# HGRN2 scores: four small levels joined in two groups of four blocks, single-key terms multiplied on GpSimd, four raw weight buffers in place of five

## The chip, the cores and the metric

One core of one Trainium2 chip runs the whole program. The metric is device time in microseconds of one launch. A core has five engines that run on their own and meet by semaphores: PE (TensorE, matmul), DVE (VectorE), ACT (ScalarE), POOL (GpSimd) and SP (SyncE, which here only issues DMAs). Each engine takes its instructions strictly in the order in which they stand in its own stream, and so does the queue of DMAs that SP issues.

## The reference, cut to what matters

A decoder layer: one combined input projection, two token mixers (mLSTM and HGRN2), a gated merge, an output projection with layer norm, and a SwiGLU feed-forward with layer norm. 512 tokens, width 1024, float32. The change is in the HGRN2 mixer: eight heads, a state of 128 keys by 128 values each.

```
def step(state, xs):                      # chunks of 16 tokens
    qc, kc, vc, lfc = xs
    a = jnp.cumsum(lfc, axis=2)
    rel = jnp.where(causal, a[:, :, :, None, :] - a[:, :, None, :, :], -jnp.inf)
    scores = jnp.einsum('bhtk,bhtsk,bhsk->bhts', qc, jnp.exp(rel), kc)
    o = (jnp.einsum('bhts,bhsv->bhtv', scores, vc)
         + jnp.einsum('bhtk,bhkv->bhtv', qc * jnp.exp(a), state))
    ...
```

Written without chunks: the score of query token t on key token s is the sum over the 128 keys of q[t] k[s] times the product of the forget gates f between s and t. The output of a head is scores times values.

## The kernel before, in words

**Weights.** Every projection takes its weight in blocks of 512 KB. `load_w` (L92) has SP issue a DMA into a raw buffer, tag `wraw`, of which there are five. `split` (L88) turns a raw block into a rounded high part `whi` (ACT) and a low remainder `wlo` (DVE), three buffers of each, and `mm3` (L83) makes three matmuls of every product: high by high, low by high, high by low. These are lines L84 to L86. A projection of 128 outputs (`proj_sub`) is 24 matmuls of 512 columns, and `natural_half` is 48 of 256 columns. The raw buffer comes free when its split is done, the split can be made when a `whi` and `wlo` pair is free, so the weight of a projection is split three projections ahead of its use.

**HGRN2 by pairs of heads.** `h_units` computes for a pair of heads (a unit, four in all) the gates f, keys K = 1 - f, queries Q, values v and output gates. K and Q are kept with the 128 keys on the partitions. `h_chain` then computes the scores of that pair while PE runs the projections of the next pair: its steps wait in a list (`defer`, `tick`), and every projection of about 5.5 us counts one tick. Eight ticks make a unit. After the last unit the gate projections of the merge take the place of the next unit.

The scores come by levels that double. Level hs joins two neighbouring blocks of hs tokens: the queries of the second block meet the keys of the first. Ahead of a level all K are multiplied by the gates up to the end of their block, and all Q by those from the start of theirs, so a level is one plain product of K and Q. After a level `h_advance` (L588) multiplies the second half of Q and the first half of K on by the block totals `tot` (L592, L593) and forms the totals of the doubled blocks (L596). The chain is:

- `h_direct_0`, `_1`, `_2`, `_3`: the diagonal and the levels of 1 and 2 tokens. There a product per key and token is formed on DVE (`h_terms`, L571, tile `e`), split into `eh` (ACT) and `el` (DVE), and summed over the 128 partitions by a matmul with ones (`h_sum`, L579).
- `h_level` for 4, 8, 16 and 32 tokens: eight matmuls of 64 columns each (L646; every float32 matmul runs as two instructions in the trace), placed into the score tile `ad` by a predicated copy on DVE (`h_place`, L604, levels 4 and 8) or by copies on ACT (L673, levels 16 and 32).
- `h_level` for 64 (L651), 128 (L657) and 256 tokens (L663).
- `h_out`: the scores times v (L692), the sum of squares of each row on ACT (tile `junk`, whose tag `sg` it shares with other small tiles), a power on POOL (L698), a scaling on DVE (L700), and one tick later the transposes (L705).

**What sets the order.** The steps are written into the program at their ticks; a scheduler then fixes the stream of each engine at build time. On the chip a late operand holds its engine and all that stands behind it there.

**After HGRN2.** `w_proj_b`, then `natural_pass` over `w_out` in two passes of eight blocks (two token tiles each, 12 matmuls of 512 columns for one block), then the feed-forward. Pool `lp` is opened after the HGRN2 pool is closed, on memory that the HGRN2 tiles held. It takes the layer norm's rows (`lng`, `lnb`) and the residual `z`, which SP loads (L756, L757, L827).

Of the kernel before, what the change touches and what calls it, by code (L numbers as in the profile page):

```python
# [29 lines left out]
O_HQ, O_HF, O_HI, O_HG, O_GA, O_GB = 8200, 9224, 10248, 11272, 12296, 13320  # L30
SOFF = [0, 512, 896, 1152]
SCOLS = 1280
WRAW = 5


@with_exitstack
def tile_hybrid_trunk(
# [40 lines left out]
    rp = pool(ctx, "rp", side="right")  # L78
# [9 lines left out]
    def split(src, hi, lo):  # L88
        return nc.scalar.copy(hi, src), nc.vector.tensor_sub(lo, src, hi.bitcast(F32))  # L89

    def load_w(src, kk, nn):
        raw = rp.tile([P, kk, nn], F32, tag="wraw", name="wraw", bufs=WRAW)  # L92
        nc.sync.dma_start(raw, src.rearrange("(k p) n -> p k n", p=P))
        return raw

# [76 lines left out]
    px = pool(st_m, "px", bufs=2, space=PSUM)  # L172
# [7 lines left out]
    for i in range(2):  # L180
        raw = mp.tile([P, 4, 264], F32, tag="dt", name="rawv", bufs=MH)
# [273 lines left out]
    for h in range(MH):  # L455
# [4 lines left out]
        for c in range(4):  # L460
            kk, qq = [feature_chunk(h, c, w) for w in range(2)]
# [16 lines left out]
        vh, vl, _ = vt_  # L478
# [34 lines left out]
    for key, gs_, w in (((1, 0), 2, 1), ((2, 0), 4, 2), ((2, 1), 4, 2), (4, 8, 4), (8, 16, 8)):
        a, n = (key[1], 1) if isinstance(key, tuple) else (0, w)
        m = hp_.tile([P, P // gs_, w], F32, name=f"mask{gs_}{a}")
        nc.gpsimd.memset(m, 1.0)
# [10 lines left out]
    def h_units(pr):  # L527

        st = dict(pr=pr, ad=ads[pr % 2])
        for name in ("f", "K", "Q", "og"):  # L530
            st[name] = hp_.tile([P, 2, T], F32, tag=name, name=name, bufs=2)
        st["v"] = hp_.tile([P, NT, 256], F32, tag="v", name="v", bufs=2)
        st["tot"] = hp_.tile([P, 1024], F32, tag="tot", name="tot", bufs=1)
        f, K, Q, og, v = (st[k] for k in ("f", "K", "Q", "og", "v"))
        for c in range(2):
            n = 2 * pr + c
            wh, wl = fetch(in_cols(O_HF + n * P), KD, P)
            ps = proj_sub(wh, wl, 0, xh, xl)
            nc.scalar.activation(f[:, c], ps, AF.Sigmoid, bias=bcol(O_HF + n * P))
            nc.scalar.activation(K[:, c], ps, AF.Sigmoid, bias=nfcol(n), scale=-1.0)  # L540
            nc.vector.tensor_scalar(f[:, c], f[:, c], omcol(n), lbcol(n), op0=OP.mult, op1=OP.add)
            nc.vector.tensor_scalar_mul(K[:, c], K[:, c], omcol(n))
# [12 lines left out]
        for g in range(2):
            nc.vector.tensor_add(v[:, 2 * g:2 * g + 2], vps[g], vb[:, None, :].to_broadcast([P, 2, 256]))
        tick()
        for c in range(2):
            n = 2 * pr + c
            wh, wl = fetch(in_cols(O_HG + n * P), KD, P)  # L560
            ps = proj_sub(wh, wl, 0, xh, xl)
            nc.scalar.activation(og[:, c], ps, AF.Sigmoid, bias=bcol(O_HG + n * P))
            tick()
        return st

    def h_terms(in0, in1, shape):
# [33 lines left out]
    def h_place(st, ps, gs_, w, key):  # L600

        dst = st["ad"].rearrange("p j (g k) -> p j g k", k=gs_)[:, :, :, gs_ - w:]
        msk = masks[key].bitcast(U32)[:, None].to_broadcast([P, 8, P // gs_, w])
        nc.vector.copy_predicated(dst, msk, ps.rearrange("p j (g k) -> p j g k", k=w))  # L604
# [27 lines left out]
    def h_direct_3(st):  # L632
        pss = [h_sum(parts, 64) for parts in st["e"]]
        for a in range(2):
            h_place(st, pss[a], 4, 2, (2, a))

    def h_level(st, hs):

        K, Q, ad = st["K"], st["Q"], st["ad"]
        if hs < 64:  # L640
            lps = psum(px, "px", (P, 8, 64))
            for c in range(2):
                for j in range(NT):
                    js = slice(j * P, (j + 1) * P)
                    mov = Q[:, c, js].rearrange("p (g two h) -> p g two h", two=2, h=hs)[:, :, 1]
                    nc.tensor.matmul(lps[:, 4 * c + j], K[:, c, js], mov, start=True, stop=True)  # L646
        elif hs == 64:
            lps = psum(px, "px", (P, 8, 64))
            for c in range(2):
                for j in range(NT):  # L650
                    nc.tensor.matmul(lps[0:64, 4 * c + j], K[:, c, j * P:j * P + 64], Q[:, c, j * P + 64:(j + 1) * P],  # L651
                                     start=True, stop=True)
        elif hs == 128:
            lps = psum(px, "px", (P, 2, 2, P))
            for c in range(2):
                for b in range(2):
                    nc.tensor.matmul(lps[:, c, b], K[:, c, 2 * b * P:(2 * b + 1) * P],  # L657
                                     Q[:, c, (2 * b + 1) * P:(2 * b + 2) * P], start=True, stop=True)
        else:
            for c in range(2):  # L660
                lps = psum(px, "px", (P, 2, 256))
                for b in range(2):
                    nc.tensor.matmul(lps[:, b], K[:, c, b * P:(b + 1) * P], Q[:, c, 256:512],  # L663
                                     start=True, stop=True)
# [3 lines left out]
        if hs < 16:
            h_place(st, lps, 2 * hs, hs, hs)
        elif hs < 64:  # L670
            for g in range(64 // hs):
                rows_ = slice(2 * hs * g, 2 * hs * g + hs)
                nc.scalar.copy(ad[rows_, :, 2 * hs * g + hs:2 * hs * (g + 1)], lps[rows_, :, hs * g:hs * (g + 1)])  # L673
        elif hs == 64:
# [52 lines left out]
    for n in range(2, KD):  # L727
        sg = hp_.tile([P, T], F32, tag="sg", name="sga", bufs=2)
# [187 lines left out]
```

## Time and profile before

| | |
|---|---|
| time, median of 3 runs | 1333.22 us (1332.94 to 1334.21) |
| the profiled execution | 1334.2 us, span 1332.5 us |
| granted TensorE clock, mean | 0.997 |
| busy: PE / DVE / ACT / POOL | 1315.9 / 753.9 / 537.0 / 41.2 us |
| HBM read, written | 138.09 MB, 2.10 MB |

The span is what the profile records from the first to the last instruction; 1.7 us lie around it. Busy time of PE counts from the start to the modelled end of a matmul, and neighbouring matmuls overlap, so the pitch from start to start is what a matmul costs in a row of them.

### The profile page before, as it was taken

What the parts mean: (1) busy time and instruction counts of PE and PEld (TensorE: products, weight loads), DVE (VectorE), ACT (ScalarE), POOL (GpSimd) and SP (SyncE); (2) the same over time, 40 slices, a digit from 0 to 9 for tenths busy, and PEclk for the clock granted to TensorE, in tenths of its full rate; (3) what the DMA queues carried; (4) which work ended last, traced back from release to release, by engine and by line L of the source; (5) the groups of instructions that cost most, each with busy time, mean ns of one, the idle gap of its engine ahead of it and who ended that gap; (6) DMA issues with size and microseconds to landing.
All of it is one profiled execution on the core that took longest, in us unless ns stands there. A gap on an engine that the chain in (4) does not pass through costs nothing.

```text
span 1332.5 us, 17405 instructions
## 1 busy us (share of the span) xinstructions
PE 1315.9 (99%) x7023; PEld 1136.1 (85%) x7023; DVE 753.9 (57%) x1140; ACT 537.0 (40%) x811; POOL 41.2 (3%) x78
## 2 busy tenths in 40 slices
PE   8999999999999999999999999999999999999997
PEld 7788889888988998889898988887898888888885
DVE  5764656566555755557586754345765433334575
ACT  4773553444342533332424333323773222233332
POOL 0000000000000002000000000000000000000001
PEclk9999999999999999999999999999999999999999
DMA  8222333233323323332232222235664343335672
GB/s 235 80 72 79 88 88 92 75 81 94 88 79 89 86 79 84 98 96 70 63 83 64 71 72 64 79 95 201 197 186 128 95 129 101 102 95 162 192 229 81
DMA packets 189424, 141.31 MB, mean 106 GB/s; under 512 B 5728, under 2 KB 178592, under 8 KB 189344
## 3 DMA queue, kind: packets, MB, share of 16 engines
q1 hardware_dynamic: 188288, 140.17, 37.0%
q8 instruction: 55, 0.90, 0.3%
q14 instruction: 25, 0.20, 0.0%
q10 hardware_dynamic: 1056, 0.03, 0.0%
HBM read 138.09 MB, written 2.10 MB: 105 GB/s over the span
## 4 chain that ended last, share of the span: by engine, by line
PE 97%; DVE 1%; ACT 1%; DMA 1%; issue 0%; POOL 0%; SPq 0%; DVEq 0%; POOLq 0%
PE pp L84 19%; PE pp L85 19%; PE pp L86 19%; PE pf L84 10%; PE pf L85 10%; PE pf L86 10%; PE px L646 2%; PE px L692 1%; PE s L85 1%; PE s L86 1%; PE s L84 1%; PE px L579 1%; DMA xn<-in_x_dram 1%; PE px L424 1%; PE px L663 1%; PE px L84 0%
## 5 line engine op out<-in xcount | busy, mean ns | idle before, releaser
L89 ACT CAST whi<-wraw 128x1024 fp32r<-128x1024 f32 x246 | 258.1, 1050 | 592.3 <-PE pp L85 253.8
L89 DVE TENSOR_TENSOR wlo<-wraw,whi 128x1024 fp32r<-128x1024 f32 x246 | 300.6, 1223 | 272.4 <-ACT whi L89 270.0
L84 PE MATMUL pp<-xh,whi 128*128 128x512 f32 x704 | 278.1, 395 | 0.0
L86 PE MATMUL pp<-xh,wlo 128*128 128x512 f32 x704 | 275.5, 391 | 0.0
L85 PE MATMUL pp<-xl,whi 128*128 128x512 f32 x704 | 275.4, 391 | 0.0
L86 PEld LDWEIGHTS pp<-xh,wlo 128*128 128x128 f32 x704 | 132.6, 188 | 28.3 <-issue 0.4
L84 PEld LDWEIGHTS pp<-xh,whi 128*128 128x128 f32 x704 | 132.7, 188 | 27.6 <-issue 1.0
L85 PEld LDWEIGHTS pp<-xl,whi 128*128 128x128 f32 x704 | 132.6, 188 | 26.2
L86 PE MATMUL pf<-x1h,wlo 128*128 128x512 f32 (+1 forms) x416 | 148.4, 357 | 0.8 <-DVE wlo L89 0.8
L84 PE MATMUL pf<-x1h,whi 128*128 128x512 f32 (+1 forms) x416 | 148.4, 357 | 0.0
L85 PE MATMUL pf<-x1l,whi 128*128 128x512 f32 (+1 forms) x416 | 148.3, 356 | 0.0
L84 PE MATMUL pp<-whi,xh 128*128 128x256 f32 x352 | 100.6, 286 | 0.0
L85 PE MATMUL pp<-wlo,xh 128*128 128x256 f32 x352 | 99.8, 284 | 0.0
L86 PE MATMUL pp<-whi,xl 128*128 128x256 f32 x352 | 99.5, 283 | 0.0
L86 PEld LDWEIGHTS pf<-x1h,wlo 128*128 128x128 f32 x416 | 78.6, 189 | 12.1 <-DVE wlo L89 1.0
L84 PEld LDWEIGHTS pf<-x1h,whi 128*128 128x128 f32 x416 | 78.6, 189 | 11.3
L85 PEld LDWEIGHTS pf<-x1l,whi 128*128 128x128 f32 x416 | 78.6, 189 | 11.3
L357 DVE SCALAR_TENSOR_TENSOR y<-u,cols,y 128x512 f32<-128x512 f32 x96 | 71.9, 750 | 6.1 <-ACT y L355 2.6
L85 PE MATMUL pf<-wlo,g 128*128 128x512 f32 x176 | 68.6, 390 | 0.0
L86 PE MATMUL pf<-whi,g 128*128 128x512 f32 x176 | 68.5, 389 | 0.0
L84 PE MATMUL pf<-whi,g 128*128 128x512 f32 x176 | 68.4, 389 | 0.0
L85 PEld LDWEIGHTS pp<-wlo,xh 128*128 128x128 f32 x352 | 67.5, 192 | 0.1
(251 smaller groups left out, 1940.3 us busy)
## 6 DMA issues: line engine op xcount, KB each, us to landing
wraw<-in_w_in_dram SPq DMA_DIRECT2D x110, 512.0 KB, 3.9
wraw<-in_w_ffn_down_dram SPq DMA_DIRECT2D x44, 512.0 KB, 3.6
wraw<-in_w_ffn_gate_dram SPq DMA_DIRECT2D x26, 512.0 KB, 3.9
wraw<-in_w_ffn_up_dram SPq DMA_DIRECT2D x26, 512.0 KB, 3.9
wraw<-in_w_proj_a_dram SPq DMA_DIRECT2D x16, 512.0 KB, 3.5
wraw<-in_w_out_dram SPq DMA_DIRECT2D x16, 512.0 KB, 3.8
wraw<-in_w_proj_b_dram SPq DMA_DIRECT2D x8, 512.0 KB, 4.3
xn<-in_x_dram SPq DMA_DIRECT2D x4, 512.0 KB, 5.0
```

Source lines behind the costliest of these rows:

```text
L84: nc.tensor.matmul(ps, lh, rh, start=start, stop=False, **kw)
L85: nc.tensor.matmul(ps, lh, rl, start=False, stop=False, **kw)
L86: nc.tensor.matmul(ps, ll, rh, start=False, stop=stop, **kw)
L89: return nc.scalar.copy(hi, src), nc.vector.tensor_sub(lo, src, hi.bitcast(F32))
L357: nc.vector.scalar_tensor_tensor(y, u[:, tap:tap + T], cwcol(tap, ch), y, op0=OP.mult, op1=OP.add)
L424: nc.tensor.transpose(tps[:, i * P:(i + 1) * P], hn[:, i, c * P:(c + 1) * P], ident)
L579: nc.tensor.matmul(ps.rearrange("p j n -> p (j n)"), ones_r, part.rearrange("p a b -> p (a b)"), start=(i == 0), stop=(i == 1))
L646: nc.tensor.matmul(lps[:, 4 * c + j], K[:, c, js], mov, start=True, stop=True)
L663: nc.tensor.matmul(lps[:, b], K[:, c, b * P:(b + 1) * P], Q[:, c, 256:512], start=True, stop=True)
L692: nc.tensor.matmul(ops[:, i], at, vc(j), start=(e == 0), stop=(e == len(terms) - 1))
```

## The change

1. **Groups.** The levels 4 and 8 become one step `h_group(4)`, the levels 16 and 32 become `h_group(16)`. A group takes four neighbouring blocks of hs tokens. K and Q stand at the state of level hs. The six pairs of blocks (target, source) need Q with the totals of none, one or two blocks between them: `h_group_targets` writes these six variants of Q into a tile `mv` (one copy on ACT, two multiplies on DVE), and the group is eight matmuls of 6 x 32 = 192 columns over four PSUM tiles. Twelve predicated copies on DVE place the result, with masks made once on POOL. Q, K and the totals are then carried over two levels at once. The copies of levels 16 and 32 on ACT are gone.
2. **Times of the steps.** Targets at ticks 3.5 and 5, groups at 4.5 and 6, the levels 64, 128 and 256 at 7, 7.5 and 8 (before 5.5, 6, 6.5), `h_out` at 8.5 and 9 (before 7 and 7.5). So `h_out` of a unit now falls on the ninth tick, where the chain of the next unit has its first: its scores times v stand on PE right ahead of the first sums of `h_direct_1` of the next unit.
3. **Terms on GpSimd.** The multiply of `h_terms` moves from DVE to POOL: five multiplies of 128 x 512 in a unit, two in `h_direct_0`, one in `h_direct_1`, two in `h_direct_2`. Its product takes the tag `sg`; `eh`, `el` share a new tag `w3` (two buffers) with `mv`.
4. **Raw buffers.** Four raw weight buffers. Once pool `lp` exists, every fifth load goes to a buffer in that pool.

```diff
-WRAW = 5
+WRAW = 4
...
+    more, loads = [], [0]
+
     def load_w(src, kk, nn):
-        raw = rp.tile([P, kk, nn], F32, tag="wraw", name="wraw", bufs=WRAW)
+        loads[0] += 1
+        if more and loads[0] % (WRAW + 1) == 0:
+            raw = more[0].tile([P, kk, nn], F32, tag="wmore", name="wraw", bufs=1)
+        else:
+            raw = rp.tile([P, kk, nn], F32, tag="wraw", name="wraw", bufs=WRAW)
...
     def h_terms(in0, in1, shape):
 
-        e = hp_.tile(shape, F32, tag="e", name="e", bufs=2)
-        eh = hp_.tile(shape, FR, tag="eh", name="eh", bufs=2)
-        el = hp_.tile(shape, FR, tag="el", name="el", bufs=2)
-        nc.vector.tensor_mul(e, in0, in1)
+        e = hp_.tile(shape, F32, tag="sg", name="e", bufs=2)
+        w3 = hp_.tile([P, 3] + shape[1:], FR, tag="w3", name="w3", bufs=2)
+        eh, el = w3[:, 0], w3[:, 1]
+        nc.gpsimd.tensor_mul(e, in0, in1)
         split(e, eh, el)
         return eh, el
...
+    def h_group_targets(st, hs):
+
+        qv = st["Q"].rearrange("p c (g b h) -> p b (c g) h", b=4, h=hs)
+        tv = st["cur"].rearrange("p (g b) -> p b g", b=4)
+        ng = 2 * T // (4 * hs)
+        tb = lambda b, n=1: tv[:, b:b + n, :, None].to_broadcast([P, n, ng, hs])
+        mv = hp_.tile([P, 6, 2 * P], F32, tag="w3", name="mv", bufs=2)
+        mvv = mv.rearrange("p b (g h) -> p b g h", h=hs)
+        nc.scalar.copy(mvv[:, 0:3], qv[:, 1:4])
+        nc.vector.tensor_mul(mvv[:, 3:5], qv[:, 2:4], tb(1, 2))
+        nc.vector.tensor_mul(mvv[:, 5:6], mvv[:, 4:5], tb(1))
+        st["mv"] = mv
+
+    def h_group(st, hs):
+
+        K, Q, ad, mv = st["K"], st["Q"], st["ad"], st["mv"]
...
+        for j2 in range(4):
+            lps = psum(px, "px", (P, 6, 2, 32))
+            lpss.append(lps)
+            for j in range(2):
+                t = 2 * j2 + j
+                nc.tensor.matmul(lps[:, :, j], K[:, t // 4, t % 4 * P:(t % 4 + 1) * P], mv[:, :, t * 32:(t + 1) * 32],
+                                 start=True, stop=True)
+        nc.vector.tensor_mul(qv[:, 1:2], qv[:, 1:2], tb(0))
+        nc.vector.tensor_mul(qv[:, 2:3], mvv[:, 3:4], tb(0))
+        nc.vector.tensor_mul(qv[:, 3:4], mvv[:, 5:6], tb(0))
+        nc.vector.tensor_mul(tv[:, 2], tv[:, 2], tv[:, 3])
+        nc.vector.tensor_mul(tv[:, 1], tv[:, 1], tv[:, 2])
+        nt_ = st["tot"][:, st["toff"]:st["toff"] + ng]
+        nc.vector.tensor_mul(nt_, tv[:, 0], tv[:, 1])
...
+        nc.vector.tensor_mul(kv[:, 0:3], kv[:, 0:3], tb(1, 3))
+        for j2 in range(4):
...
+            for b0, b1, d0 in ((0, 3, 1), (3, 5, 2), (5, 6, 3)):
+                nc.vector.copy_predicated(dst[:, d0:4], msk[:, b0:b1], src[:, b0:b1])
...
-        steps += [(t, lambda st, hs=hs: h_level(st, hs)) for t, hs in
-                  ((3.5, 4), (4, 8), (4.5, 16), (5, 32), (5.5, 64), (6, 128), (6.5, 256))]
-        steps += [(7 + 0.5 * c, lambda st, c=c: h_out(st, c)) for c in range(2)]
+        steps += [(t, lambda st, hs=hs: h_group_targets(st, hs)) for t, hs in ((3.5, 4), (5, 16))]
+        steps += [(t, lambda st, hs=hs: h_group(st, hs)) for t, hs in ((4.5, 4), (6, 16))]
+        steps += [(t, lambda st, hs=hs: h_level(st, hs)) for t, hs in ((7, 64), (7.5, 128), (8, 256))]
+        steps += [(8.5 + 0.5 * c, lambda st, c=c: h_out(st, c)) for c in range(2)]
+        steps.sort(key=lambda s_: s_[0])
...
     lp = pool(ctx, "lp", side="right")
+    more.append(lp)
```

**Three places in the streams.** First DVE in `h_direct_1` and `h_direct_2` of a middle unit, before the change. L571 is the multiply of the terms, `el` the low part of their split, L592 and L593 the advance of Q and K, L604 a placement.

```order
L89 TENSOR_TENSOR el<-e,eh 128x512 [waits Activation_49]
L622 COPY_PREDICATED ad_4702<-ident,px 128x512 [waits PE_49]
L89 TENSOR_TENSOR el<-e,eh 128x512 [waits Activation_49]
L571 TENSOR_TENSOR e<-K,Q 128x512 [waits DVE_49]
L89 TENSOR_TENSOR wlo<-wraw,whi 128x1024 [waits DMAHW3_49]
L592 TENSOR_TENSOR Q<-Q,tot 128x256x2 [waits DVE_49]
L593 TENSOR_TENSOR K<-K,tot 128x256x2
L604 COPY_PREDICATED ad_4702<-mask_4680,px 128x512 [waits PE_49]
```

The same place after the change, from the scaling of `h_out` (L749) to the second `el` of `h_direct_2`; `w_...` are tiles of tag `w3`, L607, L608 and L619 are the old L592, L593 and L604, L755 is the old L706.

```order
L749 TENSOR_TENSOR on<-px,sm 128x512 [waits Pool_49]
L89 TENSOR_TENSOR w_6169<-e,w_6169 128x512 [waits Activation_49]
L607 TENSOR_TENSOR Q<-Q,f 128x512
L608 TENSOR_TENSOR K<-K,f 128x512
L607 TENSOR_TENSOR Q<-Q,tot 128x256x2 [waits DVE_49,Pool_49]
L89 TENSOR_TENSOR w_6217<-e,w_6217 128x512 [waits Activation_49]
L608 TENSOR_TENSOR K<-K,tot 128x256x2 [waits DVE_49]
L619 COPY_PREDICATED ad_4720<-mask_4680,px 128x512 [waits PE_49]
L556 TENSOR_SCALAR f<-f,lbw 128x512 [waits Activation_49]
L755 SCALAR_TENSOR_TENSOR og<-px,cols,og 128x512 [waits PE_49]
L557 TENSOR_SCALAR K<-K,lbw 128x512 [waits Activation_49]
L89 TENSOR_TENSOR w_6222<-e,w_6222 128x512 [waits Activation_49]
```

The advance of Q now waits for POOL, since POOL reads the old Q, and the two low parts of `h_direct_2` stand behind it. What POOL does there (L586 the multiplies, L747 the power of `h_out`):

```order
L747 TENSOR_TENSOR sm<-sm,nhalf 128x4 [waits DVE_49]
L586 TENSOR_TENSOR e<-K,Q 128x512 [waits Activation_49,Pool_49]
L747 TENSOR_TENSOR sm<-sm,nhalf 128x4 [waits DVE_49]
L586 TENSOR_TENSOR e<-K,Q 128x512 [waits DVE_49,Activation_49,Pool_49]
L586 TENSOR_TENSOR e<-K,Q 128x512 [waits Activation_49]
```

The second power, for which DVE's L749 waits, now stands behind the multiply of `h_direct_1`. Before, POOL held nothing but the powers here.

The second place is SP's queue at the passage from `w_proj_b` to `w_out`, before and after:

```order
L93 DMA wraw<-in_w_proj_b_dram 128x8x128 x8
L93 DMA wraw<-in_w_out_dram 128x1024 x8
L756 DMA lng<-in_ln_g_dram 128x1024
L757 DMA lnb<-in_ln_b_dram 128x1024
L827 DMA z<-in_x_dram 128x1024 x2
L93 DMA wraw<-in_w_out_dram 128x1024 x8
```

Now the same stretch of the changed kernel's queue:

```order
L99 DMA wraw<-in_w_proj_b_dram 128x8x128 x8
L99 DMA wraw<-in_w_out_dram 128x1024 x4
L808 DMA lng<-in_ln_g_dram 128x1024
L809 DMA lnb<-in_ln_b_dram 128x1024
L879 DMA z<-in_x_dram 128x1024 x2
L99 DMA wraw<-in_w_out_dram 128x1024 x12
```

All eight blocks of the first pass stood ahead of the layer norm's loads; now four do, and the fifth goes to the buffer in `lp`.

The third place is DVE between the levels 64 and 256, before and after. The matmuls of level 256 need both results of the second pair.

```order
L592 TENSOR_TENSOR Q<-Q,tot 128x8x64 [waits PE_49]
L593 TENSOR_TENSOR K<-K,tot 128x8x64
L89 TENSOR_TENSOR wlo<-wraw,whi 128x1024 [waits DMAHW0_49,Activation_49]
L592 TENSOR_TENSOR Q<-Q,tot 128x4x128 [waits DVE_49,PE_49]
L593 TENSOR_TENSOR K<-K,tot 128x4x128 [waits DVE_49]
```

In the changed kernel it reads:

```order
L607 TENSOR_TENSOR Q<-Q,tot 128x8x64 [waits PE_49]
L608 TENSOR_TENSOR K<-K,tot 128x8x64
L89 TENSOR_TENSOR wlo<-wraw,whi 128x1024 [waits DMAHW3_49,PE_49,Activation_49]
L607 TENSOR_TENSOR Q<-Q,tot 128x4x128 [waits DVE_49,PE_49]
L608 TENSOR_TENSOR K<-K,tot 128x4x128 [waits DVE_49]
```

The rows are the same, but in PE's stream level 128 now stands right at the end of a projection and level 256 follows 11 matmuls of the next one behind it; before, 17 matmuls lay between them.

On PE a unit has two groups of eight 192-column matmuls where it had four levels of eight 64-column matmuls. The first group stands between the two halves of the value projection, the second right behind it.

More of the change, by code (lines that the diff above doesn't have):

```diff
@@ L509, in tile_hybrid_trunk, with mask_rows @@
     hbl = bp.tile([P, KD, T], FR, tag="hbl", name="hbl")
+    PAIRS = ((1, 0), (2, 1), (3, 2), (2, 0), (3, 1), (3, 0))
     masks = {}
[L513 to L516, printed above, removed]
+    def mask_rows(m, gs_, a, n, lead):
         for sg_, base in ((1, -a), (-1, a + n - 1)):
-            nc.gpsimd.affine_select(m, m, pattern=[[-gs_ * sg_, P // gs_], [0, w]],
+            nc.gpsimd.affine_select(m, m, pattern=lead + [[-gs_ * sg_, P // gs_], [0, m.shape[-1]]],
                                     compare_op=OP.is_ge, fill=0.0, base=base, channel_multiplier=sg_)
-        masks[key] = m
+    for key, gs_, w in (((1, 0), 2, 1), ((2, 0), 4, 2), ((2, 1), 4, 2)):
+        masks[key] = hp_.tile([P, P // gs_, w], F32, name=f"mask{gs_}{key[1]}")
+        nc.gpsimd.memset(masks[key], 1.0)
+        mask_rows(masks[key], gs_, key[1], 1, [])
+    for hs in (4, 16):
+        masks[hs] = hp_.tile([P, 6, 2, 32 // hs, hs], F32, name=f"mask{hs}")
+        nc.gpsimd.memset(masks[hs], 1.0)
+        for i, (_, a) in enumerate(PAIRS):
+            mask_rows(masks[hs][:, i], 4 * hs, a * hs, hs, [[0, 2]])
     ads = []
@@ L532, in h_units @@
         st["v"] = hp_.tile([P, NT, 256], F32, tag="v", name="v", bufs=2)
-        st["tot"] = hp_.tile([P, 1024], F32, tag="tot", name="tot", bufs=1)
+        st["tot"] = hp_.tile([P, 864], F32, tag="tot", name="tot", bufs=1)
         f, K, Q, og, v = (st[k] for k in ("f", "K", "Q", "og", "v"))
@@ new lines, in h_group @@
+    def h_group(st, hs):
+        K, Q, ad, mv = st["K"], st["Q"], st["ad"], st["mv"]
+        ng = 2 * T // (4 * hs)
+        mvv = mv.rearrange("p b (g h) -> p b g h", h=hs)
+        qv = Q.rearrange("p c (g b h) -> p b (c g) h", b=4, h=hs)
+        kv = K.rearrange("p c (g b h) -> p b (c g) h", b=4, h=hs)
+        tv = st["cur"].rearrange("p (g b) -> p b g", b=4)
+        tb = lambda b, n=1: tv[:, b:b + n, :, None].to_broadcast([P, n, ng, hs])
+        lpss = []
+        for j2 in range(4):
[12 more added lines that the diff above has]
+        nc.vector.tensor_mul(nt_, tv[:, 0], tv[:, 1])
+        st["cur"] = nt_
+        st["toff"] += ng
+        nc.vector.tensor_mul(kv[:, 0:3], kv[:, 0:3], tb(1, 3))
+        for j2 in range(4):
+            dst = ad[:, 2 * j2:2 * j2 + 2].rearrange("p j (g b h) -> p b (j g) h", b=4, h=hs)
+            src = lpss[j2].rearrange("p b j (g h) -> p b (j g) h", h=hs)
+            msk = masks[hs].rearrange("p b j g h -> p b (j g) h").bitcast(U32)
+            for b0, b1, d0 in ((0, 3, 1), (3, 5, 2), (5, 6, 3)):
+                nc.vector.copy_predicated(dst[:, d0:4], msk[:, b0:b1], src[:, b0:b1])
@@ L637, in h_level @@
     def h_level(st, hs):
         K, Q, ad = st["K"], st["Q"], st["ad"]
[L640 to L647, printed above, removed]
+        if hs == 64:
@@ L667, in h_level @@
         h_advance(st, hs)
[L668 to L674, printed above, removed]
+        if hs == 64:
             nc.scalar.copy(ad[0:64, :, 64:128], lps[0:64])
```

## The prediction

> **What bounds the kernel now.** The page first, its busy times and its chain that ended last; then what PE waited for.
>
> ```profile
> PE 1315.9 (99%) x7023; PEld 1136.1 (85%) x7023; DVE 753.9 (57%) x1140; ACT 537.0 (40%) x811; POOL 41.2 (3%) x78
> PE 97%; DVE 1%; ACT 1%; DMA 1%; issue 0%; POOL 0%; SPq 0%; DVEq 0%; POOLq 0%
> PE px L200 <- DMA xn<-in_x_dram: 5.7, 2, 4.8
> PE pf L84 <- DVE sgb L741: 0.9, 1, 0.9
> PE pf L86 <- DVE wlo L89: 0.8, 1, 0.8
> ```
>
> PE is the bound from start to end; beside the load of x at the start it waits 0.9 us once, at the passage to `w_out`, and 0.8 us once. In HGRN2 it waits for nothing. So PE work that goes is time that goes, and each new wait of PE adds in full. Sixty microseconds of HGRN2, columns PE, PEld, DVE, ACT, POOL, clock, DMA:
>
> ```profile
> 600.00:660.00 60.00, 60.00 (x382) 53.80 (x381) 39.90 (x61) 20.88 (x46) 2.04 (x2) 1.00 0.24 64
> ```
>
> DVE is busy two thirds of the time, so the chains that PE waits for have room, but not without limit. Next, the price of a level on PE, from the time line (start, length, instruction).
>
> ```profile
> 621.16 0.28 PE L86 MATMUL pp<-whi,xl 128*128 128x256 f32 x1
> 621.28 0.28 PE L84 MATMUL pp<-whi,xh 128*128 128x256 f32 x1
> 621.45 1.97 PE L646 MATMUL px<-Q,K 128*128 128x64 f32 x16
> 623.23 0.36 PE L85 MATMUL pp<-wlo,xh 128*128 128x256 f32 x1
> 623.43 0.28 PE L86 MATMUL pp<-whi,xl 128*128 128x256 f32 x1
> 623.55 0.29 PE L84 MATMUL pp<-whi,xh 128*128 128x256 f32 x1
> ```
>
> A level's 16 instructions hold PE for 623.23 - 621.45 = 1.78 us, 0.111 us each. At both ends the pitch is longer than the 0.12 us of this stage, 0.17 ahead and 0.20 behind: 0.13 us more. What a width costs:
>
> ```profile
> 630.40 1.05 PE L657 MATMUL px<-Q,K 128*128 128x128 f32 x8
> 631.21 0.48 PE L85 MATMUL pp<-xl,whi 128*128 128x512 f32 x1
> 635.18 1.89 PE L663 MATMUL px<-Q,K 128*128 128x256 f32 x8
> 636.90 0.61 PE L692 MATMUL px<-v,ad 128*128 128x128 f32 x4
> 637.35 0.39 PE L692 MATMUL px<-v,a 128*128 128x128 f32 x2
> ```
>
> 128 columns cost 0.81 / 8 = 0.10 to 0.45 / 4 = 0.11 us, no more than 64 do; 256 cost 1.72 / 8 = 0.215. A level of 64 columns pays for 128.
>
> **The change part by part.**
>
> *Groups on PE.* 192 columns lie halfway between 0.11 and 0.215: 0.163 us, bounds those two. A group is 16 x 0.163 = 2.61 us and 0.13 at its ends, 2.74; the two levels it replaces are 2 x 1.91 = 3.82 where their ends lie in a stage like the one shown, and 0.1 less each where the block begins at a projection's end. I take 0.9 us for a group, eight groups: **-7.2 us** (bounds: -14 at 0.11, -0.5 at 0.215). The other steps of PE keep their instructions.
>
> *Groups on DVE and ACT.* DVE loses five multiplies, two placements and four advances a unit, gains the targets, the advances in parts and 24 small placements. Rows of the same kind (start, length):
>
> ```profile
> 631.49 0.69 DVE L592 TENSOR_TENSOR Q<-Q,tot 128x512 f32<-128x512 f32 x1 [0.29 <-PE px L657]
> 632.10 0.68 DVE L593 TENSOR_TENSOR K<-K,tot 128x512 f32<-128x512 f32 x1
> 612.81 0.70 DVE L604 COPY_PREDICATED ad<-mask,px 128x512 f32<-128x512 uint32 x1
> 654.69 0.53 DVE L541 TENSOR_SCALAR f<-f,lbw 128x512 f32<-128x512 f32 x1
> 655.13 0.48 DVE L542 TENSOR_SCALAR K<-K,lbw 128x512 f32<-128x512 f32 x1
> ```
>
> A multiply of 512 elements has a pitch of 0.61 us, a placement in runs of four takes 0.70. In proportion to the elements that is about 9.8 us off and 11.4 on. ACT trades six small copies for two larger ones. PE does not wait for sums of work but for chains, so these cost nothing of themselves; what is left of their cover is counted behind the next walk.
>
> *`h_out` and `h_direct_2`.* Here the change adds waits: DVE's advance of Q for POOL's multiplies, with both `el` of `h_direct_2` behind it, for which PE's sums wait. The rows:
>
> ```profile
> 639.05 0.48 PE L84 MATMUL pp<-xh,whi 128*128 128x512 f32 x1
> 640.51 0.17 DVE L697 TENSOR_SCALAR sm<-sm 128x4 f32<-128x4 f32 x1 [3.01 <-ACT junk L696]
> 641.82 0.69 DVE L700 TENSOR_TENSOR on<-px,sm 128x512 f32<-128x512 f32 x1 [1.14 <-POOL sm L698]
> 654.13 0.39 PE L84 MATMUL pp<-xh,whi 128*128 128x512 f32 x1
> 659.58 0.40 PE L579 MATMUL px<-eh,ones 128*128 128x512 f32 x1
> 602.35 0.40 PE L579 MATMUL px<-eh,ones 128*128 128x512 f32 x1
> 603.02 1.32 DVE L604 COPY_PREDICATED ad<-mask,px 128x512 f32<-128x512 uint32 x1 [2.12 <-PE px L579]
> 1323.83 0.74 DVE L871 SCALAR_TENSOR_TENSOR z<-z,lsm,lnb 128x512 f32<-128x512 f32 x1
> 1324.24 1.46 POOL L866 TENSOR_TENSOR z<-z,lng 128x512 f32<-128x512 f32 x1 [1.12 <-ACT z L865]
> 1325.78 1.27 POOL L867 TENSOR_TENSOR z<-z,lnb 128x512 f32<-128x512 f32 x1
> ```
>
> Count from the start of `h_out` on PE in a middle unit. PE: 40 instructions of 0.111 are 4.45, the first sums four matmuls of 0.23 to 5.4, a projection of 24 matmuls (659.58 - 654.13 = 5.45, 0.227 each) to 10.85, one pair of sums and eight transposes to 12.1, a projection to 17.6; the last of the four sums then needs the second `el` at 18.3. POOL: the slot of the next multiply comes free with the squares of the second head, one microsecond behind 4.45 (640.51 - 639.05 less a little), say 5.5; the multiply takes 1.27 by the row of the plain add, then the power (about 1.05 with its wait, by the 1.14 that L700 idled) to 7.85. DVE: `on` to 8.5, `el` to 9.1, Q and K at 0.6 and 0.7 to 10.4. POOL's two multiplies of `h_direct_2`: to 13.05. DVE: Q 0.6, `el` 0.6, K 0.6, the placement 1.1, the gate's scaling 0.45, `og` 0.7, K's scaling 0.4, the second `el` 0.7: 18.2. That is 0.1 us ahead of PE. Three POOL multiplies lie in this chain, and they read Q and K at a stride where both rows of the trace read whole rows. I take 1.45 us each, nearest to the longer row: 0.4 us late, in the two units that have both an `h_out` ahead and a further HGRN2 unit beside them (the first has no `h_out`, the last has two placements fewer ahead of its `el`): **+0.8 us**, from 0 to 3.6 at 2 us each.
>
> Carried on, PE needs the second group's K at 38.3 (18.6, a projection, 48 matmuls of 0.12, the first group 2.74, 48 matmuls). DVE has by the rows about 17.6 us of work from 18.2 up to that K, four `wlo` among it: 35.8, and up to 1.5 more where its advance of the next unit's Q waits for POOL's multiplies of `h_direct_0`. One microsecond of room is left: nothing added.
>
> [...] No run here shows a strided read on POOL.
>
> *Level 256 nearer to level 128.* The split of the next weight starts at a projection's end, and DVE makes `wlo` ahead of the advance:
>
> ```profile
> 635.20 1.04 ACT L89 CAST whi<-wraw 128x1024 fp32r<-128x1024 f32 x1 [3.12 <-PE pp L85]
> 636.27 1.23 DVE L89 TENSOR_TENSOR wlo<-wraw,whi 128x1024 fp32r<-128x1024 f32 x1 [1.08 <-ACT whi L89]
> ```
>
> From a projection's end: `whi` at once, `wlo` 1.07 later, 1.14 of pitch, Q 0.6, K 0.7: 3.5 us. PE comes to level 256 after 0.81 + 0.1 + 11 x 0.2275 = 3.4 us. Late by 0.1 to 0.2, four times: **+0.6 us** (0 to 1.2). Before, 17 matmuls covered it.
>
> *Four raw buffers.* While projections run, a load is taken up four projections of 5.45 us after its issue, and even the slow landing below is 8.2 us: one buffer fewer is hidden there. At the passage to `w_out` it is not: the fifth block now stands behind `lng`, `lnb` and two `z`, which wait for the last low part of the merge, and each is 512 KB. The rows of SP, the landing times of loads issued then, and PE's first matmul of `w_out`:
>
> ```profile
> 916.30 0.33 SPq L756 DMA_DIRECT2D lng<-in_ln_g_dram  x1
> 917.16 0.99 SPq L827 DMA_DIRECT2D z<-in_x_dram  x2
> 919.29 0.33 SPq L93 DMA_DIRECT2D wraw<-in_w_out_dram  x1
> z<-in_x_dram SPq DMA_DIRECT2D x1, 512.0 KB, 8.6
> wraw<-in_w_out_dram SPq DMA_DIRECT2D x1, 512.0 KB, 8.2
> 913.90 0.47 PE L84 MATMUL pf<-whi,mxh 128*128 128x512 f32 x1 [0.88 <-DVE sgb L741]
> ```
>
> The fifth block would be issued at 917.16 + 0.99 = 918.2. By the 8.2 us of the load issued a microsecond later into the same traffic it lands at 926.4; `whi` and `wlo` (1.07 + 1.23) make it 928.7. PE has four blocks of 12 x 0.2275 = 2.73 us, to 913.90 + 10.9 = 924.8, and 0.3 more ahead of the first matmul with `wlo`. **+3.6 us**, once; the blocks behind land together and are hidden. The old traffic had one more load ahead of these, so it may land up to 2 us sooner, or, with three further blocks close behind, 1.5 later: 1.5 to 5 us. It could be nothing only if loads overtook those issued before.
>
> *Sum.* -7.2 + 0.8 + 0.6 + 3.6 = -2.2 us. The profiled execution took 1334.2, of which 1332.5 are span; it would take 1332.0. The median of the runs is 1.0 lower, 1333.22, so the forecast is **1331.0 us**, a gain of 0.17%. About 0.2% (2.7 us) is what a measurement of this kernel can tell from no change: 1330.5 to 1335.9.
>
> **The rivals.**
>
> *The loads hide and the chains hold.* If the fifth block lands by 923, none of the 3.6 comes, and -7.2 + 0.6 + 0 to 0.8 leaves about -6: **1327**. For it: the DMA engines are busy 0.24 of the time in HGRN2, so they have rate to spare. Against: 8.2 and 8.6 us of landing just there.
>
> *Slower: POOL's multiplies hold DVE up.* Units two and three pay three times what a multiply takes above 1.3 us. At 1.8 us each the term is 6 x 0.5 = 3 and the gain is gone; above 2.3 the kernel is slower by over 0.2%. At 2.5 us it is 7, the two multiplies of the next unit's `h_direct_0` push the second group's K past its 1 us of room by about 1.5 in all, and the sum is +5.5: **1338.5**. For it: two rows of one pair of instructions, L871 and L866, overlap by 0.33 us, and that multiply took 0.19 longer than the add behind it; and DVE is busy two thirds of the time in this stage. Against: in the chain above DVE stands idle while POOL multiplies. [...]
>
> *192 columns cost as much as 256.* Then 128 instructions give back 128 x 0.052 = 6.7 us, and -2.2 becomes +4.5: **1337.7**. Against: 128 columns cost half of 256.
>
> **How the numbers follow.** The forecast's case 0.46, its own range 1328.5 to 1333.8 by the bounds of the load wait and the chain; loads and chains hidden 0.30; POOL 0.17; width 0.07. Faster by over 0.2%: 0.28 of the hidden case and 0.09 of the forecast's, 0.37. Slower: 0.17 and 0.06, 0.23. Within: 0.40. The range leaves out the far ends of the last two: 1327 to 1337.
>
> **What would show it.** Right: L680 at 0.16 us of pitch, PE waiting 3 to 4 us at the fifth block of `w_out` for `wlo`, and tenths of a microsecond at the sums of `h_direct_2` and at level 256. Wrong: no wait of PE in `w_out`; multiplies on POOL near 2 us or more; waits of PE at the groups themselves, which would say that the targets come late; a wait of projections for `wlo`, which would say that DVE has become the bound of the stage.

## The result, and the profile after

The changed kernel is slower: 1345.19 us median (1344.26 to 1347.10, four runs) against 1333.26 for the kernel before (also four runs), a ratio of 1.0086 with a 95% interval of 1.0072 to 1.0100. The forecast was 1331.0 us with a range of 1327 to 1337; the result lies outside it.

The page of the changed kernel, its busy times and its chain:

```profile
PE 1314.5 (98%) x6895; PEld 1130.5 (84%) x6895; DVE 763.2 (57%) x1232; ACT 536.3 (40%) x795; POOL 82.0 (6%) x118
PE 93%; DVE 3%; DMA 1%; ACT 1%; POOL 1%; issue 0%; SPq 0%; DVEq 0%; POOLq 0%; ACTq 0%
```

PE has 128 instructions fewer and is still the bound, but its share of the chain fell from 97% to 93%: it waits. What for, in the view of waits (waiting line, releaser, total us, times, longest):

```profile
PE pf L84 <- ACT whi L89: 13.4, 1, 13.4
PE px L206 <- DMA xn<-in_x_dram: 5.5, 2, 4.6
PE px L594 <- DVE w L89: 1.5, 2, 0.8
PE pf L86 <- DVE wlo L89: 0.7, 1, 0.7
```

The second and fourth stood in the profile before at about the same size (5.7 and 0.8). The third is the forecast's wait at the sums of `h_direct_2`. The first is the loss, and it is one wait. The time line of the changed kernel there: SP's issues, ACT's casts, DVE's last split of the merge and PE's first matmuls of `w_out`:

```profile
881.57 16.65 SPq L99 DMA_DIRECT2D wraw<-in_w_out_dram  x4
914.50 0.33 SPq L808 DMA_DIRECT2D lng<-in_ln_g_dram  x1
914.88 0.43 SPq L809 DMA_DIRECT2D lnb<-in_ln_b_dram  x1
915.35 0.90 SPq L879 DMA_DIRECT2D z<-in_x_dram  x2
916.29 12.56 SPq L99 DMA_DIRECT2D wraw<-in_w_out_dram  x4
907.63 0.62 ACT L89 CAST mxh<-sgb 128x512 fp32r<-128x512 f32 x1 [4.82 <-DVE sgb L793]
913.07 0.62 ACT L89 CAST mxh<-sgb 128x512 fp32r<-128x512 f32 x1 [4.82 <-DVE sgb L793]
923.92 2.94 ACT L89 CAST whi<-wraw 128x1024 fp32r<-128x1024 f32 x3 [10.23 <-DMA wraw<-in_w_out_dram]
913.72 0.69 DVE L89 TENSOR_TENSOR mxl<-sgb,mxh 128x512 fp32r<-128x512 f32 x1 [0.68 <-ACT mxh L89]
925.02 1.22 PE L84 MATMUL pf<-whi,mxh 128*128 128x512 f32 x2 [13.43 <-ACT whi L89]
```

Four blocks of `w_out` were issued between 881.57 and 898.2, the last of them landed 3.5 us after its issue, and so all four were there at 911.6, when PE finished `w_proj_b`. Yet ACT cast none of them until a load landed at 923.8, the one issued at 916.29 behind `lng`, `lnb` and two `z`. Then it cast three at once. So the late load is not the fifth block of `w_out`: it is the first, and the four that lay ready are blocks two to five.

In the kernel before, the casts of `w_out` alternated with the high parts of the merge:

```profile
907.44 1.05 ACT L89 CAST whi<-wraw 128x1024 fp32r<-128x1024 f32 x1 [3.18 <-PE pp L85]
909.08 0.62 ACT L89 CAST mxh<-sgb 128x512 fp32r<-128x512 f32 x1 [0.59 <-DVE sgb L742]
```

The number could have been had without a run. `load_w` counts all loads. The page has 246 casts `whi`, one for each load:

```profile
L89 ACT CAST whi<-wraw 128x1024 fp32r<-128x1024 f32 x246 | 257.9, 1050 | 578.1 <-PE pp L85 209.4
```

Of these 52 belong to the feed-forward's gate and up, 44 to its down projection, 16 to `w_out`, which leaves 134 ahead. The first block of `w_out` is load 135, and 135 divides by five. The order of ACT's instructions in the changed kernel, the last casts of the merge and the first two of `w_out`, shows it too:

```
L89 CAST mxh<-sgb 128x512 [waits DVE_49] x4
L89 CAST whi<-wraw 128x1024 [waits DVE_49,DMAHW0_49,PE_49,Pool_49]
L89 CAST whi<-wraw 128x1024 [waits PE_49]
```

The first cast of `w_out` stands behind the last `mxh`. It waits for DVE and POOL beside its DMA, which the next one does not; its load went to a buffer in `lp`, on memory that the HGRN2 tiles held. SP's rows, on which the section on the change and the prediction rest, name the tensor and not the block; both say "the fifth", and that is wrong.

The wait has a second price, the granted clock. Columns PE, PEld, DVE, ACT, POOL, then the clock, DMA share and GB/s, changed kernel:

```profile
911.00:914.00 3.00, 0.58 (x3) 0.16 (x1) 1.66 (x3) 0.62 (x1) 0.00 (x0) 1.00 0.00 0
920.00:925.00 5.00, 0.00 (x0) 0.00 (x0) 0.00 (x1) 1.08 (x2) 0.00 (x0) 0.50 0.57 233
925.00:928.00 3.00, 2.94 (x6) 1.94 (x7) 3.00 (x3) 1.86 (x2) 0.00 (x0) 0.50 0.31 44
928.00:932.00 4.00, 4.00 (x18) 3.26 (x18) 1.62 (x2) 1.05 (x1) 0.00 (x0) 0.97 0.82 301
```

A clock of 0.50 is called half clock here. PE begins `w_out` at half clock and keeps it for 3.2 us, to 928.26. From its first matmul there to the end of the span the changed kernel takes 1345.3 - 925.02 = 420.3 us, the kernel before 1332.5 - 913.90 = 418.6: 1.7 us, put down to the slow start.

**The account of the profiled executions.** Up to the first sum of HGRN2 the changed one is 3.4 us later (593.40 against 590.02), with nothing changed there but the buffers; the granted clock shows why. That sum and the stretch of clock in the kernel before, then in the changed one:

```profile
590.02 0.40 PE L579 MATMUL px<-eh,ones 128*128 128x512 f32 x1
```

```profile
60.00:70.00 10.00, 10.00 (x44) 7.47 (x45) 4.39 (x7) 9.91 (x16) 2.75 (x7) 1.00 0.22 55
```

```profile
593.40 1.09 PE L594 MATMUL px<-w,ones 128*128 128x512 f32 x4
```

```profile
60.00:70.00 10.00, 10.00 (x27) 6.62 (x27) 4.61 (x7) 9.91 (x16) 2.55 (x7) 0.66 0.20 53
```

0.34 of 10 us is 3.4. From that sum to the end of `w_proj_b` (925.02 - 13.43 = 911.59 and 913.90 - 0.88 = 913.02) it gains 318.2 - 323.0 = -4.8. Then the wait, 13.4 - 0.9 = +12.5, and +1.7 behind it: 3.4 - 4.8 + 12.5 + 1.7 = 12.8, the difference of the spans, 1345.3 - 1332.5. The medians lie 11.9 apart, 2.5 more than the 9.4 that is left without the lower clock at 60 us. Three of the four runs have the mean clock of the profiled one, 0.990, so that lower clock is probably in most of them; only one was profiled.

### The profile page after: what moved, and what is told of

It is laid out like the page before. It is cut to its first block, busy times and chain, and to the rows that moved or that the text cites. A ratio compares the mean times of both kernels' runs of the same rounds, so it can differ in the third digit from the quotient of the medians.

```text
span 1345.3 us, 17266 instructions
## 1 busy us (share of the span) xinstructions
PE 1314.5 (98%) x6895; PEld 1130.5 (84%) x6895; DVE 763.2 (57%) x1232; ACT 536.3 (40%) x795; POOL 82.0 (6%) x118
## 4 chain that ended last, share of the span: by engine, by line
PE 93%; DVE 3%; DMA 1%; ACT 1%; POOL 1%; issue 0%; SPq 0%; DVEq 0%; POOLq 0%; ACTq 0%
PE pp L84 18%; PE pp L85 18%; PE pp L86 18%; PE pf L85 10%; PE pf L84 10%; PE pf L86 10%; PE px L680 2%; PE s L86 1%; PE s L85 1%; PE s L84 1%; PE px L741 1%; PE px L718 1%; DMA wraw<-in_w_out_dram 1%; PE px L430 1%; DMA xn<-in_x_dram 1%; POOL e L586 0%
```

## The experiments

The theory: the gain of the groups is there, and the numbering of the loads, which gives the late buffer to the first block of `w_out`, costs it back with 9 us on top. The rivals: four buffers or the loads' traffic are slow whichever block is late; and POOL's multiplies, or DVE, hold the stage up. Of the kernel before, 16 or 17 runs lie beside each group of experiments, with a median of 1334.3.

**The fifth block in place of the first (e1_fifth).** This is the case that the prediction worked out.

```diff
-        if more and loads[0] % (WRAW + 1) == 0:
+        if more and loads[0] % (WRAW + 1) == WRAW:
```

> The changed kernel with one number altered: the load that goes to the buffer in the pool of layer norm is the fifth block of w_out in place of the first. Theory (the first block of w_out, load 135, is the one that went there; it waited for the last low part of the merge, and PE waited 13.4 us for it): PE's wait ahead of w_out falls back to about 0.9, and the fifth block lands near 923.9 as the first one did; PE would come to it at 912.5 + 10.9 = 923.4, and its high and low part are ready at 925.0 and 926.25: waits of about 2.5 us together at the fifth block. The slow clock behind the long wait (1.7 us) goes too. 1345.2 - 12.5 - 1.7 + 2.5 = 1333.5. Rival (the loads in that place are slow of themselves, whichever block is among them, or the four buffers cost the time earlier): 1342 or more, with 10 us of waits left in w_out.

Measured: 1335.29 us, ratio 1.0004 (0.9990 to 1.0017), 10 us less than the changed kernel. PE's rows:

```profile
908.15 0.47 PE L84 MATMUL pf<-whi,mxh 128*128 128x512 f32 x1 [0.88 <-DVE sgb L792]
922.99 2.07 PE L84 MATMUL pf<-whi,mxh 128*128 128x512 f32 x4 [3.72 <-ACT whi L89]
```

The theory holds: the wait ahead of `w_out` is 0.88 again, and the one at the fifth block is 3.72, where the prediction had 3.6 and this expectation 2.5. The slow clock behind it was missing from both. The clock from the wait's start on, in the same kernel:

```profile
919.00:922.00 3.00, 0.27 (x2) 0.00 (x0) 0.00 (x0) 0.11 (x1) 0.00 (x0) 1.00 0.93 380
923.00:925.00 2.00, 2.00 (x5) 1.61 (x6) 2.00 (x2) 1.83 (x2) 0.00 (x0) 0.50 0.00 0
```

From its first matmul of `w_out` to the end this execution takes 1332.1 - 908.15 = 424.0 us, 5.4 more than the kernel before: the wait of 3.7 and 1.6 beside it. So even as the prediction had it, with the fifth block late, the change is no gain: 1335.3 against 1334.3.

**The extra buffer only behind the first pass (e2_late).** `more.append(lp)` moves from the opening of `lp` to the end of the first pass of `w_out`.

```diff
-    more.append(lp)
...
         tick(0)
+        if not more:
+            more.append(lp)
```

> The changed kernel, but the pool of layer norm takes loads only after the first pass of w_out, so that this pass runs through the four raw buffers and seven of its blocks stand ahead of the layer norm's loads. Theory: no wait beyond 0.9 us at the passage, the slow clock behind it gone: 1345.2 - 12.5 - 1.7 = 1331.0. From the two profiles alone, without the 3.3 us that the profiled execution of the changed kernel lost to a lower clock between 60 and 90 us, the groups leave -4.8: 1333.2 - 4.8 = 1328.5. Which of the two it is tells whether that lower clock belongs to the four buffers (1331) or to single executions (1328.5). Rival (the passage isn't the cause, four buffers are): 1340 or more.

Measured: 1329.09 us, ratio 0.9965 (0.9952 to 0.9978): the change with its passage mended is faster than before. PE's first row of `w_out`:

```profile
911.13 0.47 PE L84 MATMUL pf<-whi,mxh 128*128 128x512 f32 x1 [0.88 <-DVE sgb L792]
```

From there to the end it takes 1329.7 - 911.13 = 418.6 us, as the kernel before: the 1.7 us are gone with the wait. Three runs at a mean granted clock of 0.997 took 1328.1 to 1328.5, one at 0.996 took 1329.7, and the two at 0.995 took 1331.4 and 1331.5. So both numbers of the expectation occur. Four buffers do not always bring the lower clock at 60 us: the profiled execution here has 0.66 over 60 to 70 us, that of e4_dve_terms below, with the same buffers, has 1.00. The kernel before also has runs of both kinds (of the 17 beside a later group, four at 0.994 took 1337.7 to 1338.2 and 13 at 0.996 or 0.997 took 1332.9 to 1334.9), but none of its runs at 0.994 was profiled. Whether four buffers make it more frequent is not shown.

**The buffers alone (e3_buffers_alone).** The kernel before with `WRAW = 4`, the counter and `more.append(lp)` of the change, and nothing else of it.

> The kernel before with part four of the change alone: four raw buffers, and every fifth load to the pool of layer norm once it exists. The first block of w_out is again load 135. Theory: 13.4 - 0.9 = 12.5 of wait and 1.7 of slow clock behind it: 1333.3 + 14.2 = 1347.5. Rival (the wait comes of the changed HGRN2 stage, which ends at another time): under 1337.

Measured: 1353.26 us, ratio 1.0147 (1.0133 to 1.0160). PE's first row of `w_out`:

```profile
930.23 1.22 PE L84 MATMUL pf<-whi,mxh 128*128 128x512 f32 x2 [13.45 <-ACT whi L89]
```

The clock behind it:

```profile
930.00:935.00 5.00, 4.74 (x10) 3.31 (x11) 3.50 (x3) 2.07 (x3) 0.00 (x0) 0.50 0.43 126
```

The same wait without any of the groups: the rival falls. The size was 5.8 us over the expectation. The profile puts 1.1 of it to a half clock of 5.4 us in place of 3.2, 3.7 to the time ahead of HGRN2 (its first sum stands at 593.76, and the clock is 0.66 over 60 to 70 us), and the kernel before beside it stood at 1334.3, 1.0 above the 1333.3 of the expectation; all four runs had a clock of 0.989.

**A shorter wait (e9_shorter_wait).** As in e1_fifth, but `lnb` is loaded behind the first pass, so that 512 KB less stand ahead of that block.

```diff
-    g1, b1 = ln_rows(ln1_g, ln1_b)
+    g1 = ln_row(ln1_g, "lng")
...
         tick(0)
+        if ts_[0] == 0:
+            b1 = ln_row(ln1_b, "lnb")
```

> As e1_fifth, with one row of layer norm (lnb, 512 KB) loaded behind the first pass of w_out, so that one load fewer stands ahead of the fifth block. Theory (the half clock of 1.7 us' cost behind the 3.7 us wait came about 3.5 us after the wait's start, so a wait under that stays free of it): the block lands 1.5 to 2 us earlier, PE waits about 2 us and the clock stays at 1.00: 3.1 to 3.4 us less than e1_fifth, of which the wait is 1.7. Rival (any wait of PE over a microsecond brings the half clock): 1.7 us less, with 0.50 in the granted clock behind the wait.

Measured: 1332.73 us, ratio 0.9986 (0.9976 to 0.9997), 2.6 us less than with the wait of 3.72 by the medians, 3.1 by the lowest runs (1330.10 and 1333.19). The wait, and in the second fence the clock through it:

```profile
922.63 1.20 PE L84 MATMUL pf<-whi,mxh 128*128 128x512 f32 x4 [2.22 <-ACT whi L89]
```

```profile
922.00:924.00 2.00, 1.31 (x5) 0.79 (x6) 1.39 (x2) 2.00 (x3) 0.00 (x0) 1.00 0.22 90
924.00:926.00 2.00, 2.00 (x9) 1.66 (x10) 2.00 (x2) 0.47 (x1) 0.00 (x0) 1.00 0.57 119
```

The clock stands at 1.00 behind the wait of 2.2 us here, and at 0.50 behind the 3.72 of e1_fifth, where it fell 3.2 us after the wait's start (the expectation has about 3.5). No wait between the two was measured. The rival falls.

**The terms back on DVE (e4_dve_terms)**, on the kernel with the mended passage:

```diff
-        nc.gpsimd.tensor_mul(e, in0, in1)
+        nc.vector.tensor_mul(e, in0, in1)
```

> As e2_late, with the single terms multiplied on VectorE in place of GpSimd. Theory (PE's two waits of 0.77 us at the sums of h_direct_2 come of GpSimd's multiplies, 1.5 us each, in a chain where VectorE stands idle; on VectorE one takes 0.6 to 0.7): both waits go, 1.5 us less than e2_late. Rival (VectorE, busy two thirds of the time and with 20 multiplies or 13 us more, becomes late for the groups or for the low parts of weights): 1 to 6 us more than e2_late, with waits of PE at the groups (L680) or at projections.

Measured: 1327.52 us, ratio 0.9958 (0.9944 to 0.9971), 1.6 less than on GpSimd; the intervals overlap. The trace decides: PE's two waits at L594 are gone and no other came. A multiply takes 0.69 us on DVE (L571 in the kernel before). The sums of `h_direct_2` in units two and three, first in the changed kernel, then here:

```profile
667.09 0.86 PE L594 MATMUL px<-w,ones 128*128 128x512 f32 x3
668.71 0.50 PE L594 MATMUL px<-w,ones 128*128 128x512 f32 x1 [0.77 <-DVE w L89]
729.56 0.86 PE L594 MATMUL px<-w,ones 128*128 128x512 f32 x3
792.04 1.26 PE L594 MATMUL px<-w,ones 128*128 128x512 f32 x4
```

```profile
662.52 1.09 PE L594 MATMUL px<-w,ones 128*128 128x512 f32 x4
723.94 1.09 PE L594 MATMUL px<-w,ones 128*128 128x512 f32 x4
```

A unit with such a wait (the second is behind the row of 729.56, not shown) takes 792.04 - 729.56 = 62.48 us, without it 723.94 - 662.52 = 61.42: a wait of 0.77 costs 1.06. The wait counts from the modelled end of the matmul ahead; by the starts the fourth sum is 0.92 late (668.71 against 667.09 and three pitches of 0.23). DVE carries the 20 multiplies unnoticed. So moving them to GpSimd relieved an engine that nobody waited for, and lengthened a chain.

**GpSimd's multiplies alone (e6_pool_alone).** The kernel before with the reverse of that line.

> The kernel before, with the single terms multiplied on GpSimd, and nothing else of the change. Theory (a multiply takes 1.3 alone to 2.3 us beside VectorE's work; the chain of h_direct_2 has a tenth of a microsecond of room): waits of PE at the sums, 0.8 us in each of two to three units, 1.5 to 2.5 us more than before: 1335 to 1336 where before is 1333.3. Rival (the order of the kernel before leaves more room there, so that the waits need the moved steps as well): 1333.3, no wait at the sums.

Measured: 1336.40 us, ratio 1.0017 (1.0005 to 1.0029), 2.1 us more. The size was as expected, the place wasn't. There is no wait at the sums, as the rival had it, but six short ones stand at the levels, behind DVE's advance:

```profile
PE px L646 <- DVE K L593: 1.2, 6, 0.2
```

A unit takes 729.12 - 665.19 = 63.93 us, 0.76 more than in the kernel before, and three units have two such waits each.

**Level 256 back by half a projection (e5_level256)**, to stand ahead of the first `h_out` as it did before, with the terms on DVE:

```diff
-        steps += [(t, lambda st, hs=hs: h_level(st, hs)) for t, hs in ((7, 64), (7.5, 128), (8, 256))]
+        steps += [(t, lambda st, hs=hs: h_level(st, hs)) for t, hs in ((7, 64), (7.5, 128), (8.5, 256))]
```

> As e4_dve_terms, with level 256 set back by half a projection, to stand right ahead of the first h_out, as in the kernel before. Theory (level 256 comes 0.27 us late behind the split of a weight and costs another mode change of PE, 0.19 us; 0.45 us a unit): 4 x 0.45 = 1.8 us less than e4_dve_terms, the two L718 rows' gap ahead back to 0.23. Rival (h_out then waits for ScalarE's copies of level 256, which it reads from its third tile on): no gain, or up to 2 us more, with waits of PE at L741.

Measured: 1326.83 us, ratio 0.9945 (0.9927 to 0.9962), the lowest median of all and faster than both kernels. The gain on the kernel with the terms on DVE, 0.7 by the medians, is inside the intervals. The trace shows it: level 256 in the changed kernel with the row ahead, then here, then two units here.

```profile
644.16 0.39 PE L85 MATMUL pp<-xl,whi 128*128 128x512 f32 x1
644.65 1.97 PE L718 MATMUL px<-Q,K 128*128 128x256 f32 x8
```

```profile
643.91 0.39 PE L86 MATMUL pp<-xh,wlo 128*128 128x512 f32 x1
644.14 1.89 PE L718 MATMUL px<-Q,K 128*128 128x256 f32 x8
663.54 1.09 PE L594 MATMUL px<-w,ones 128*128 128x512 f32 x4
724.59 1.09 PE L594 MATMUL px<-w,ones 128*128 128x512 f32 x4
```

The gap ahead is 0.23 in place of 0.49, and a unit takes 61.05 in place of the 61.42 of e4_dve_terms: 0.37 four times, 1.5 us. The "mode change" of 0.19 us in the expectation is the pitch behind the block in the changed kernel, 0.42 us (646.27 to 646.69) where the matmuls of a projection have 0.23; the trace does not show what makes it longer. `h_out` does not wait for the copies. The two profiled executions have the same span, 1324.2; this one came to its first sum of HGRN2 1.4 us later (590.21 against 588.83) and made that up.

**Level 256 back, terms on GpSimd (e8_pool_level256).**

> As e2_late (terms on GpSimd) with level 256 set back as in e5_level256. Theory: e2_late less 1.8 us, and the two waits of 0.77 us at the sums of h_direct_2 remain. Rival (without the gap at level 256 PE is earlier at the sums, and they wait longer by as much): e2_late less 0.9, with waits of about 1.2 us.

Measured: 1328.31 us, ratio 0.9954 (0.9938 to 0.9969), 0.8 less than with level 256 where the change has it; by the medians alone that can't be told from no gain. In the trace the two waits are 0.77 each as before, as the theory has it, and from the first sum to the end it takes 1.4 us less than e2_late (736.2 against 737.6).

**No fifth buffer at all (e7_four)**, with the terms on DVE.

> As e4_dve_terms, with four raw buffers to the end and no fifth at all. Theory (a block of 512 KB lands 3.6 us after its issue in an ordinary stretch and is wanted four blocks, 11 us or more, later): as e4_dve_terms within 1 us. Rival (the passages to the next passes want the fifth): 2 to 6 us more, with waits of PE for low or high parts of weights.

Measured: 1327.60 us, ratio 0.9951 (0.9934 to 0.9967), against 1327.52 with it. The extra buffer earns nothing that these runs can show.

**From the first sum of HGRN2 to the end.** Counted so, the lower clock at 60 us is left out. The profiled executions take 742.5 us (before), 744.7 (terms on GpSimd alone), 737.6 (e2_late), 735.4 (terms back on DVE) and 734.0 (level 256 back as well): the groups with their moved steps are worth 8.5, the terms on GpSimd cost 2.2 and the place of level 256 costs 1.4.

## Why the prediction was wrong

**The step that failed** is the one on the four raw buffers: "the fifth block now stands behind `lng`, `lnb` and two `z`". The first block does. That a load behind these four is late was right, and for the fifth block the term was close (3.6 against 3.72 measured). But with a late fifth block PE has four others to work on, and with a late first block nothing: the wait runs from the end of `w_proj_b`, 12.5 us more than before in place of 3.6. A second term was left out: 1.7 us for the half clock behind the wait, which a late fifth block brings too (1.6). The runs show a clock of 0.50 behind 3.7 and 13.4 us of wait in `w_out` and 1.00 behind 2.2; it fell 3.0 (changed kernel), 3.2 (e1_fifth) and 5.2 us (e3_buffers_alone) after the wait's start, and the half clock lasted 3.2, 2.9 and 5.4 us behind its end. What sets these times is not shown: the wait of 4.8 us for x, with which the span of the kernel before opens, has a clock of 1.00 over 0 to 20 us.

**Groups.** Right in kind, and the estimate of the width nearly so: 16 instructions of 192 columns cost 2.47 us, a pitch of 0.154 where 0.163 was taken. The first group in the changed kernel, with the row behind it:

```profile
617.80 2.77 PE L680 MATMUL px<-mv,K 128*128 128x192 f32 x16
620.27 0.41 PE L84 MATMUL pp<-whi,xh 128*128 128x256 f32 x1
```

The same sums in two units of the kernel before:

```profile
665.51 0.40 PE L579 MATMUL px<-eh,ones 128*128 128x512 f32 x1
728.68 0.40 PE L579 MATMUL px<-eh,ones 128*128 128x512 f32 x1
```

The kernel before takes 728.68 - 665.51 = 63.17 us a unit, the version with level 256 back and no wait 61.05: 2.1 four times, -8.4 against -7.2. The rival that 192 columns cost as much as 256 falls with it.

**`h_out` and `h_direct_2`.** The walk along the chain named the wait, its place and its two units. It gave 0.4 us each, and PE waited 0.77 and lost 1.06: 2.1 us in place of 0.8, inside its bounds. (The upper bound of 3.6 is a slip: at 2 us a multiply the walk gives 2 x (3 x 0.73 - 0.1) = 4.2.) The rows of POOL:

```profile
563.13 1.29 POOL L586 TENSOR_TENSOR e<-K,Q 128x512 f32<-128x512 f32 x1 [19.32 <-DVE Q L565]
655.17 1.53 POOL L586 TENSOR_TENSOR e<-K,Q 128x512 f32<-128x512 f32 x1 [0.88 <-ACT junk L745]
660.52 3.02 POOL L586 TENSOR_TENSOR e<-K,Q 128x512 f32<-128x512 f32 x2 [2.70 <-DVE K L608]
616.26 2.33 POOL L586 TENSOR_TENSOR e<-K,Q 128x512 f32<-128x512 f32 x1 [5.98 <-DVE tot L685]
```

In this chain the three multiplies take 1.53 and twice 1.51, where 1.45 was taken, and the slot of the first comes free 5.75 us after the start of `h_out` on PE (655.17 - 649.42), where the walk had 5.5: together 0.45 of the 0.5 us by which the fourth sum is later than walked. On whole rows, with DVE idle beside it (563.13), a multiply takes 1.29; the two of `h_direct_2`, which read pairs that lie 16 bytes apart, take 0.22 more each, again with DVE idle beside them. The 2 us each of the upper bound and the 2.5 of the rival were the author's assumptions: no run shows them in this chain, though multiplies elsewhere take up to 2.38; the one of 2.33 ran beside a `wlo` of DVE (616.13 to 617.35).

**Level 256.** Right in place, too small: the gap grew by 0.26 us in each unit, where the walk had 0.1 to 0.2, and a unit lost 0.37. The other 0.11 is probably the one more pair of ends that it has as a block of its own; that was not measured apart. It is 1.5 us in all against 0.6, over the bound of 1.2.

**The sum** with the measured terms: -8.4 + 2.1 + 1.5 + 12.5 + 1.7 = 9.4, and the profiled execution has 12.8 - 3.4 = 9.4 beside the clock dip. The three terms of HGRN2 add to -4.8 where -5.8 was forecast; that they come so close is in part luck, since the larger gain of the groups covers part of two terms that were too small. The passage to `w_out`, +14.2 in place of +3.6, turned the sign.

## What to carry to other kernels

When a buffer is assigned by a running count, work out which load gets it at the place where it matters, and look at who consumes it: the queue's rows name the tensor only, the consumer's waits tell the block. A late load costs its lateness less the work that stands ahead of it, so the first block of a stage is the worst one to delay: 13.4 us of wait for the first block of `w_out` here, 3.72 for the fifth. Ask of a long wait of PE what the clock does behind it: in `w_out` a stretch of half clock cost 1.6 to 2.8 us behind waits of 3.7 to 13.5, in which the clock fell 3.0 to 5.2 us after the start, and a wait of 2.2 had none. An engine that is busy two thirds of the time but that nobody waits for needs no relief, least of all by a slower engine in a chain (1.51 to 1.53 us a multiply in place of 0.69).

## What was not expected of the hardware

Half clock also comes with PE at work: in the profiles of before and after alike the granted clock is 0.83 over 40 to 50 us, and in the profiled executions of three versions (the changed kernel, e2_late, e3_buffers_alone) 0.66 over 60 to 70, with PE busy 9.9 to 10 of 10 us. It is 0.50 over 44 to 46 in the kernel before and over 62 to 68 in the changed one. By the missing share of the clock it costs 1.7 and 3.4 us. The three executions with the second have mean clocks of 0.990, 0.995 and 0.989, so it probably makes most of the spread of the runs; its cause stays open, and no experiment was made on it.

A DVE instruction beside a multiply on POOL took longer. DVE's scaling of 128 x 4, 0.17 us in the kernel before, took 1.17 in the changed one and ended with the multiply of POOL that ran from 655.17 to 656.70. The next two units show the same (1.17 and 0.97), and with the terms on DVE it takes 0.15 to 0.17. Why is not shown. The first of the three rows:

```profile
655.56 1.17 DVE L746 TENSOR_SCALAR sm<-sm 128x4 f32<-128x4 f32 x1
```
